# Second feed-forward products as seven block products on one core of a Trainium2 chip

## The chip, the cores and the metric

The kernel runs on one core of one Trainium2 chip. The metric is the device time of one execution in microseconds (us). Before the change the median of three runs is 2907.16 us (2906.84 to 2908.7).

Engines are named as in the profile: PE is TensorE's matmuls, PEld its weight loads, DVE is VectorE, ACT is ScalarE, POOL is GpSimd, SP is SyncE, whose queue issues nearly all DMAs of this kernel.

## The reference

One layer of a decoder trunk on 1024 prompt tokens and 64 sample tokens (8 sequences of 8), all in float32: a half-step feed-forward, a token mixing (pooling branch and a state-space branch), a second half-step feed-forward, and a final norm. What the change touches are the two feed-forwards:

```python
def swiglu(x, w_in, w_out):
    gu = x @ w_in                                   # (tokens, 1024) @ (1024, 2 * 2816)
    g, u = gu[..., :D_FF], gu[..., D_FF:]
    return (jax.nn.silu(g) * u) @ w_out             # (tokens, 2816) @ (2816, 1024)

x = x + 0.5 * swiglu(rmsnorm(x, norm_ffn1[l]), ffn1_w_in[l], ffn1_w_out[l])
...                                                 # token mixing
x = x + 0.5 * swiglu(rmsnorm(x, norm_ffn2[l]), ffn2_w_in[l], ffn2_w_out[l])
```

The product with w_in is called the first product below, the one with w_out the second.

## The kernel before

**Layout.** Activations lie with features on the 128 partitions and tokens along the free dimension. Tokens are split into two halves: half 0 has 512 (prompt), half 1 has 576 (512 prompt and the 64 sample tokens). A tile of one half is one block of 128 features. The hidden width of 2816 is 22 blocks (NFF), the model width 1024 is 8 (KD).

**Precision.** A float32 product is made of three matmuls in a rounded float32 type: the operand and the weight are each split into a high and a low part, and high x high, high x low and low x high are added up in PSUM. `split` (line 354) makes the parts of an operand: ScalarE copies the high part, VectorE subtracts. `load_w` (line 272) loads 4 blocks of weights, 256 KB, and does the same for them (lines 295 and 296). `part` (line 306) does this ahead for chosen chunks and stores the two parts in DRAM, from where load_w later only loads them.

**First products.** `ffn` (line 650) runs one feed-forward. The first few hidden blocks go by `ffn_in_plain` (line 613). All others go by `ffn_in` (line 538), which makes the gate block and the up block of one hidden block by seven products in place of eight; its weights need sums of weight blocks that GpSimd makes (line 438), then the split (lines 444 and 445). The result of one hidden block and one half, g, is stored in DRAM (`hdram`; lines 579, 609 and 627). Its tiles come from a tag of 17 buffers (`fx`, line 109): two results, and t and v, which hold products that were taken out of PSUM. The last hidden block is done half after half.

**Second products.** The loop that begins under `finish(side)` in `ffn` does half 0, then half 1. It loads the 22 operand tiles of the half (`hr`, `hp`, line 682), splits them, and goes over the 8 output blocks m: for each it loads w_out four row blocks at a time and does 22 x 3 matmuls for each piece of the half (half 0 is one piece of 512 columns, half 1 two pieces of 288). PSUM has eight banks; six of them have the tag "pd", which these products and the first ones share. An output block leaves PSUM by one VectorE instruction for each piece (line 700), which adds half of it to the residual tile loaded from `xspill`. The first two output blocks go together, and their weights were prepared by `part` during the first products (`out01`). After half 0 the chain that follows (`after`) is started: after the first feed-forward this is the norm of half 0 for the token mixing; after the second it is the final norm and output, whose first part (`half`) starts when four output blocks are there. The same follows for half 1.

**What sets the order.** Instructions are put on the engines' queues by a scheduler when the program is built; it takes them in program order where their operands and buffers are free. Side work is written as generators ("chains"): each pause names a number of microseconds of TensorE time after which it goes on, and `tick()` in the matmul loops steps the chains that are due. `high_priority` lets a group of instructions be taken earlier: weight splits by HP (40), emptying of PSUM by HP_EV (60).

## Time and profile before

The profiled execution spans 2904.2 us from the first to the last instruction; the median of the runs is 2907.16 us, 2.96 us longer, which is what lies around the span. All times of stages and single instructions are from this one execution.

| stage of the profiled execution (us from the start of the span) | length |
|---|---|
| first feed-forward: plain blocks and operands, 0 to 104.9 | 104.9 |
| first feed-forward: first products, 104.9 to about 524.9 | 420 |
| first feed-forward: second products, half 0, 524.9 to 649.08 | 124.18 |
| first feed-forward: second products, half 1, 649.08 to 790.83 | 141.75 |
| token mixing, to 2146.5 | 1355.7 |
| second feed-forward: plain blocks, to 2207.4 | 60.9 |
| second feed-forward: first products, to 2618.7 | 411.3 |
| second feed-forward: second products, half 0, to 2748.0 | 129.30 |
| second feed-forward: second products, half 1, to 2888.6 | 140.60 |
| last final norm and output, to the end | 15.6 |

How to read the lines shown below: a line of the table by stage has the stretch, its length, then for each engine its busy time and the number of its instructions, then the granted clock of TensorE (1.00 is full), the share of time in which the 16 DMA engines were busy, and GB/s moved. A line of a group has the line of the program, the engine, the operation, output<-inputs by the program's names, shapes, the count; behind the bar the busy time in us and the mean of one in ns; behind the second bar the time that the engine sat idle just before them, and what ended it. All matmuls have the line of the helper that issues them (164), so they are told apart by the names of their tiles: pw for first products, po for second ones. The recorded length of a matmul includes its passage through the array; how often one starts is read from the starts of a row of them.

### The profile page before, as it was taken

The numbers are of one execution on the slowest core, as the hardware profiler recorded it, in microseconds if no ns is written. First come the engines' busy times: TensorE is split into PE (matmuls) and PEld (weight loads), VectorE is DVE, ScalarE is ACT, GpSimd is POOL, SyncE is SP. The second block draws the span as 40 slices with busy tenths as digits, with TensorE's granted clock in tenths as the row PEclk, the third lists the DMA queues.
The fourth block names the chain that finished last, engine by engine and source line by source line (L and its number), as shares of the span: only waits on it lengthen the run. The fifth ranks groups of instructions, "written<-read, shape, count | busy, mean of one in ns | idle before, by whom it ended". The sixth has DMA issues, their size and how long they took to land. (4 is left out here: it accounts for less than half of the span.)

```text
span 2904.2 us, 52545 instructions
## 1 busy us (share of the span) xinstructions
PE 2823.4 (97%) x19306; PEld 2609.3 (90%) x19306; DVE 1701.8 (59%) x2702; ACT 1365.2 (47%) x3004; POOL 1003.0 (35%) x1088
## 2 busy tenths in 40 slices
PE   7999999999999999999999999899999999999998
PEld 6999999789989999999988887678999999997898
DVE  6665555534384586766766777765665544453432
ACT  5454444323354565554556566566234444442322
POOL 5444444000132365564622343332244444440000
PEclk9999999999999999999999999999999999999999
DMA  4575554856445455543376677786764522236642
GB/s 120 166 225 188 170 171 129 280 178 200 125 129 165 151 182 169 190 136 121 106 248 206 197 232 232 256 256 184 255 231 144 163 92 82 79 114 206 220 155 73
DMA packets 520803, 502.84 MB, mean 173 GB/s; under 512 B 36565, under 2 KB 365129, under 8 KB 520537
## 3 DMA queue, kind: packets, MB, share of 16 engines
q1 hardware_dynamic: 520528, 499.47, 54.0%
q8 instruction: 152, 2.49, 0.4%
q14 instruction: 107, 0.87, 0.1%
q10 hardware_dynamic: 16, 0.00, 0.0%
HBM read 356.53 MB, written 143.05 MB: 172 GB/s over the span
## 5 line engine op out<-in xcount | busy, mean ns | idle before, releaser
L164 PE MATMUL pw<-X,wh 128*128 128x288 f32 (+2 forms) x2832 | 625.5, 310 | 2.8 <-ACT t L590 2.6
L164 PEld LDWEIGHTS pw<-X,wh 128*128 128x128 f32 x2832 | 461.3, 189 | 24.5 <-ACT t L590 3.0
L164 PE MATMUL pw<-X,wl 128*128 128x288 f32 (+1 forms) x1644 | 472.9, 288 | 0.9 <-DVE wl L445 0.9
L164 PE MATMUL pw<-hl,wh 128*128 128x256 f32 (+1 forms) x1536 | 391.5, 328 | 0.7 <-ACT t L566 0.7
L445 DVE TENSOR_TENSOR wl<-s,wh 128x512 fp32r<-128x512 f32 x288 | 227.7, 791 | 234.4 <-ACT wh L444 210.7
L164 PE MATMUL pw<-hi,wh 128*128 128x288 f32 x1120 | 331.1, 296 | 0.5 <-ACT t L600 0.5
L164 PE MATMUL pw<-hi,wl 128*128 128x288 f32 x1120 | 330.0, 295 | 0.0
L164 PE MATMUL pw<-lo,wh 128*128 128x288 f32 x1120 | 329.6, 294 | 0.0
L438 POOL TENSOR_TENSOR s<-wraw,wraw 128x512 f32<-128x512 f32 x144 | 196.5, 1365 | 357.3 <-DVE wl L445 253.0
L164 PEld LDWEIGHTS pw<-X,wl 128*128 128x128 f32 x1644 | 311.1, 189 | 1.1 <-DVE wl L445 1.1
L164 PE MATMUL pw<-hl,wl 128*128 128x256 f32 x1072 | 300.0, 280 | 0.0
L296 DVE TENSOR_TENSOR wl<-wraw,wh 128x512 fp32r<-128x512 f32 x208 | 149.6, 721 | 251.1 <-ACT wh L295 248.8
L164 PEld LDWEIGHTS pw<-hl,wh 128*128 128x128 f32 x1536 | 258.8, 189 | 21.7 <-ACT t L566 1.4
L295 ACT ACTIVATE wh<-wraw 128x512 fp32r<-128x512 f32 x208 | 125.5, 605 | 314.6 <-PE po L164 241.7
L444 ACT ACTIVATE wh<-s 128x512 fp32r<-128x512 f32 x288 | 181.0, 630 | 162.4 <-PE pw L164 138.1
L445 DVE TENSOR_TENSOR wl<-wraw,wh 128x512 fp32r<-128x512 f32 x216 | 168.2, 779 | 137.2 <-ACT wh L444 125.6
L164 PEld LDWEIGHTS pw<-hi,wh 128*128 128x128 f32 x1120 | 210.5, 188 | 7.4 <-ACT t L600 1.3
L164 PE MATMUL po<-hh,wh 128*128 128x288 f32 (+1 forms) x800 | 210.8, 323 | 3.6 <-ACT hh L356 3.3
L164 PE MATMUL po<-hr,wh 128*128 128x288 f32 (+1 forms) x800 | 210.9, 323 | 0.0
L164 PE MATMUL po<-hh,wl 128*128 128x288 f32 (+1 forms) x800 | 210.6, 322 | 0.0
L164 PEld LDWEIGHTS pw<-lo,wh 128*128 128x128 f32 x1120 | 210.6, 188 | 0.0
L164 PEld LDWEIGHTS pw<-hi,wl 128*128 128x128 f32 x1120 | 210.1, 188 | 0.4 <-DVE wl L445 0.4
(381 smaller groups left out, 6239.6 us busy)
## 6 DMA issues: line engine op xcount, KB each, us to landing
wraw<-in_ffn_w_in_dram SPq DMA_DIRECT2D x188, 256.0 KB
wh<-part SPq DMA_DIRECT2D x156, 256.0 KB
wl<-part SPq DMA_DIRECT2D x156, 256.0 KB
wraw<-in_w_in_dram SPq DMA_DIRECT2D x144, 256.0 KB
wraw<-in_ffn_w_out_dram SPq DMA_DIRECT2D x120, 256.0 KB
part<-ph SPq DMA_DIRECT2D x80, 256.0 KB
part<-pr SPq DMA_DIRECT2D x80, 256.0 KB
ab<-acsd SPq DMA_DIRECT2D x64, 256.0 KB
```

Source lines behind the costliest of these rows:

```text
L164: T.matmul(out, lhsT, rhs, start=start, stop=stop, skip_group_check=free)
L295: S.activation(wh, raw, AF.Copy)
L296: V.tensor_tensor(wl, raw, wh.bitcast(F32), op=ALU.subtract)
L438: G.tensor_tensor(t, a, b, op=op)
L444: S.activation(wh, a, AF.Copy)
L445: V.tensor_tensor(wl, a, wh.bitcast(F32), op=ALU.subtract)
```

## The change

Hidden blocks are paired: block 2k is the even, block 2k+1 the odd one, eleven pairs (NKK). The 1088 tokens are cut anew into two sides of 544: side 0 is half 0 and the first 32 tokens of half 1, side 1 the other 544. The output blocks are cut into the first four (y = 0) and the last four (y = 1). The product is then 2 x 2 blocks by 2 x 2 blocks, and is done by seven products of block sums, in the order 2, 5, 1, 7, 4, 3, 6, each of 11 row blocks, 4 output blocks and 2 pieces of 272 columns:

- The sums of operands (for products 6, 7, 1, 4, 3) are made by GpSimd in the first products' stage as soon as both blocks of a pair are there for both halves (`sums`), and stored in DRAM (`xq`); the operands of 2 and 5 are stored there straight from g. The result of a hidden block is stored in hdram only by `ffn_in_plain`, from where `sums` loads it again.
- The weight sums (two blocks of w_out each for products 1, 2, 5, 6, 7; one block for 3 and 4) are made by GpSimd when they are needed, and then split (`second_weights`). One load has two row blocks of 256 columns.
- Each group of 2 output blocks has four PSUM banks. A finished bank is added to every residual tile that it belongs to (INTO2: one to two target blocks, with a sign), in two pieces where it lies over the border of the halves. All 16 residual tiles (8 output blocks, 2 halves) stay in fx buffers from product 2 on.
- The operands of the next product are loaded and split during the current one (`fetch_x`); the low parts for products 3 and 6 are made by GpSimd.
- `after` of half 0 is called when product 4 is done, `half` of half 1 after product 3, `after` of half 1 at the end. For the second feed-forward `half` is no longer used for half 0; its final norm and output are one chain.
- The preparation of w_out chunks (`out01`) is gone from both feed-forwards; of the pause before the norm of half 0 (HN_AT), 25, 3 is left.

The diff, without some of the glue:

```diff
-HN_AT, HN_PACE = 25.0, 2.0
+HN_AT, HN_PACE = 3.0, 2.0
+NKK, NQ, NA = NFF // 2, 272, 32
+ORDER2 = "2517436"
+BLOCKS2 = {"1": ((0, 0), (1, 1)), "2": ((0, 1), (1, 1)), "3": ((0, 0),), "4": ((1, 1),), "5": ((0, 0), (1, 0)),
+           "6": ((0, 1), (0, 0)), "7": ((1, 0), (1, 1))}
+MINUS2 = "67"
+INTO2 = {"1": ((0, 0, 1), (1, 1, 1)), "2": ((1, 0, 1), (1, 1, -1)), "3": ((0, 1, 1), (1, 1, 1)),
+         "4": ((0, 0, 1), (1, 0, 1)), "5": ((0, 0, -1), (0, 1, 1)), "6": ((1, 1, 1),), "7": ((0, 0, 1),)}
+IN_PAIRS = "214"
+LO_POOL = "36"
+X_AT, X_PACE = 5.0, 2.2
+SUM_PACE = 1.5
...
-                dma(hdram[0][ff], g[:, : 2 * n])
+                produced(ff, 0, g)
...
-                dma(hdram[h][ff], o["g"][:, : 2 * n])
+                produced(ff, h, o["g"])
...
         dma(hdram[h][ff], g[:, : NTOK[h]])
+        produced(ff, h, g, True)
+
+    def produced(ff, h, g, spilled=False):
+        made[ff, h] = None if spilled else g
+        kk, odd = divmod(ff, 2)
+        if odd:
+            if h == 1:
+                dma(xq["5"][kk], g[:, NA : NA + 2 * NQ])
+        elif h == 0:
+            dma(xq["2"][kk][:, :512], g[:, :512])
+        else:
+            dma(xq["2"][kk][:, 512 : 512 + NA], g[:, :NA])
+        if odd and all((2 * kk + i, q) in made for i in range(2) for q in HALVES):
+            summing.append(start(sums(kk), SUM_PACE))
+
+    def sums(kk):
...
+        def both(p, out, x0, x1, y, op):
+            G.tensor_tensor(out[:, a], x0[:, a], y[:, b0], op=op)
+            G.tensor_tensor(out[:, s], x1[:, :NA], y[:, b1], op=op)
+            dma(xq[p][kk], out[:, :n])
+
+        both("6", fx(name="s6"), e0, e1, e1, ALU.add)
+        yield SUM_PACE
+        both("7", fx(name="s7"), o0, o1, o1, ALU.add)
+        yield SUM_PACE
+        both("1", fx(name="s1"), e0, e1, o1, ALU.add)
+        yield SUM_PACE
+        G.tensor_tensor(o0[:, a], o0[:, a], e0[:, a], op=ALU.subtract)
+        G.tensor_tensor(o0[:, s], o1[:, :NA], e1[:, :NA], op=ALU.subtract)
+        dma(xq["4"][kk], o0[:, :n])
+        yield SUM_PACE
+        G.tensor_tensor(e1[:, NA : NA + n], e1[:, NA : NA + n], o1[:, NA : NA + n], op=ALU.subtract)
+        dma(xq["3"][kk], e1[:, NA : NA + n])
...
+    def second_weights(wo, p, kp, n2, m0):
+        raws = []
+        for x, y in BLOCKS2[p]:
+            raw = sp.tile([P, 4 * P], F32, tag="wraw", bufs=N_RAW, name=nm("wraw"))[:, : n2 * 2 * P]
+            c0 = (4 * y + m0) * P
+            dma(raw.rearrange("p (k c) -> p k c", c=2 * P),
+                wo.rearrange("(k t p) c -> p t k c", t=2, p=P)[:, x, kp : kp + n2, c0 : c0 + 2 * P])
+            raws.append(raw)
+        with tc.high_priority(hp[0]):
+            if len(raws) > 1:
+                s = stage["p"].tile([P, 4 * P], F32, tag="wsum", bufs=N_S, name=nm("ws"))[:, : n2 * 2 * P]
+                G.tensor_tensor(s, raws[0], raws[1], op=ALU.subtract if p in MINUS2 else ALU.add)
...
+            S.activation(wh, s, AF.Copy)
+            V.tensor_tensor(wl, s, wh.bitcast(F32), op=ALU.subtract)
...
+    def second(wo, after, half):
...
+                dma(t[:, :n], xq[p][kk])
+                S.activation(a[:, :n], t[:, :n], AF.Identity)
+                (G if p in LO_POOL else V).tensor_tensor(t[:, :n].bitcast(F32R), t[:, :n], a[:, :n].bitcast(F32), op=ALU.subtract)
...
+        def add(pt, m, side, c, sign):
+            if side:
+                to = [(1, NA + NQ * c, 0, NQ)]
+            else:
+                to = [(0, 0, 0, NQ)] if c == 0 else [(0, NQ, 0, NQ - NA), (1, 0, NQ - NA, NA)]
+            for h, at, of, w in to:
+                o = C[m, h][:, at : at + w]
+                V.scalar_tensor_tensor(o, pt[:, of : of + w], 0.5 * sign, o, op0=ALU.mult, op1=ALU.add)
...
+        for at, p in enumerate(ORDER2):
+            finish(ahead)
+            if at + 1 < len(ORDER2):
+                last = at + 2 == len(ORDER2)
+                ahead = start(fetch_x(ORDER2[at + 1], range(NKK), 1.6 if last else X_PACE), 14.0 if last else X_AT)
+            for m0 in (0, 2):
+                pts = [[psum("pd", "po") for _ in range(2)] for _ in range(2)]
+                for kp in range(0, NKK, 2):
+                    n2 = min(2, NKK - kp)
+                    W2 = second_weights(wo, p, kp, n2, m0)
+                    for j in range(2):
+                        for k in range(n2):
+                            xh, xl = X[p][kp + k]
+                            for i, (w, x) in enumerate(((0, xh), (0, xl), (1, xh))):
+                                for c in range(2):
+                                    mm(pts[j][c][:, :NQ], W2[w][:, k, j * P : (j + 1) * P], x[:, c * NQ : (c + 1) * NQ],
+                                       start=kp + k == 0 and i == 0, stop=kp + k == NKK - 1 and i == 2)
                             tick()
...
+                with tc.high_priority(HP_EV):
+                    for j in range(2):
+                        for c in range(2):
+                            for y, side, sign in INTO2[p]:
+                                add(pts[j][c], 4 * y + m0 + j, side, c, sign)
+            if p == "4":
+                after(0, [C[m, 0] for m in range(KD)])
+            if p == "3" and half:
+                half(1, [C[m, 1] for m in range(KD)])
+        after(1, [C[m, 1] for m in range(KD)])
```

In product 2 the residual tiles are loaded, four output blocks in each of its two groups, and the sums of the last pair are finished there.

More of the change, by code (lines that the diff above doesn't have):

```diff
@@ L669, in ffn, with fetch_x @@
             finish(side)
-        for h in HALVES:
-            N = NTOK[h]
-            parts = [], []
-            for k in range(NFF):
-                own = k < 4 if h == 0 else not half and k >= NFF - 2
-                if 4 <= k < 4 + N_PAIR and (h == 0 or half):
+        second(wo, after, half)
+    def second_weights(wo, p, kp, n2, m0):
[11 more added lines that the diff above has]
+            else:
+                s = raws[0]
+            wh, wl = (sp.tile([P, 4 * P], F32R, tag=t, bufs=N_W, name=nm(t))[:, : n2 * 2 * P] for t in ("wh", "wl"))
+            S.activation(wh, s, AF.Copy)
+            V.tensor_tensor(wl, s, wh.bitcast(F32), op=ALU.subtract)
+        return [t.rearrange("p (k c) -> p k c", c=2 * P) for t in (wh, wl)]
+    def second(wo, after, half):
+        X, C = {p: [] for p in ORDER2}, {}
+        n = 2 * NQ
+        def fetch_x(p, kks, pace):
+            for kk in kks:
+                if p in IN_PAIRS and kk < N_PAIR:
                     a, t, _ = pair(576, "hp")
@@ L1722, in half2 @@
     def half2(g, xt):
+        finish(fin[-1])
         xf.append(xt)
@@ L1726, in after2, with whole @@
     def after2(g, xt):
+        if g == 0:
+            def whole():
+                xf.append(xt)
+                yield from final_head(0)
+                yield from final(0)
+            fin.append(start(whole(), 2.0))
+            return
         finish(fin[-1])
         fin.append(start(final(g)))
-    ffn(ffn2_w_in[0], ffn2_w_out[0], prep2, after2, half=half2, side=part(ffn2_w_out[0], out01))
+    ffn(ffn2_w_in[0], ffn2_w_out[0], prep2, after2, half=half2)
     for c in fin:
```

57 lines of the change are left out of this document (31 added, 26 removed).

## The prediction

> **What bounds the kernel now.** I read the page first, then the time split at the borders of the feed-forward stages, then the rows of the second products.
>
> ```profile
> span 2904.2 us, 52545 instructions
> ...
> PE 2823.4 (97%) x19306; PEld 2609.3 (90%) x19306; DVE 1701.8 (59%) x2702; ACT 1365.2 (47%) x3004; POOL 1003.0 (35%) x1088
> ...
> PEclk9999999999999999999999999999999999999999
> ```
> ```profile
> core 0: us, PE busy (x) PEld busy (x) DVE busy (x) ACT busy (x) POOL busy (x), PEclk, DMA share, GB/s
> ...
> 104.90:511.00 406.10, 404.98 (x2725) 380.11 (x2724) 234.46 (x385) 193.98 (x425) 185.67 (x173) 1.00 0.55 175
> ...
> 2207.40:2605.00 397.60, 397.25 (x2662) 373.30 (x2661) 203.67 (x323) 172.83 (x361) 185.17 (x175) 1.00 0.34 106
> ...
> 2888.60:2904.20 15.60, 2.47 (x21) 1.85 (x18) 6.50 (x15) 5.54 (x14) 1.17 (x1) 0.70 0.44 151
> ```
>
> TensorE is busy 97% of the span at full granted clock. In the two "first product" stages (104.9 to 511 and 2207.4 to 2605) it idles 1.1 and 0.35 us, while POOL has over half its time free. The second products stand in the answer for the tile po alone:
>
> ```profile
> 524.90:649.08 124.18, 121.88 (x529) 98.66 (x529) 4.82 (x7) 1.00 0.69 220
> 649.08:790.83 141.75, 140.91 (x1057) 140.42 (x1055) 6.42 (x15) 1.00 0.55 168
> 2618.70:2748.00 129.30, 126.65 (x554) 101.51 (x553) 5.52 (x8) 1.00 0.62 199
> 2748.00:2888.60 140.60, 139.25 (x1032) 137.56 (x1031) 5.84 (x15) 1.00 0.40 125
> sum 535.83, PE 528.70 PEld 478.15 DVE 22.60; mean PE 132.17 PEld 119.54 DVE 5.65
> ```
>
> Both second products together take 535.8 us and are full of matmuls. So whatever takes matmuls away here comes off the span, unless another resource then ends last. By code one product issues 22 x 8 x 3 = 528 matmuls of 512 columns (first half) and 1056 of 288 (second half); a few records are missing or stand over a border.
>
> **The matmuls.** The change does 7 block products of 11 x 4 x 3 x 2 = 264 matmuls, each 272 columns wide: 1848 per feed-forward, 3696 in all, in place of 3168. Their spacing is taken between two widths of the trace. The timeline shows 30 matmuls of 512 columns in a row, the first and the last of them here; the chain that ended last shows a run of 486 of 288 columns:
>
> ```profile
> 642.28 0.39 PE L164 MATMUL po<-hh,wh 128*128 128x512 f32 x1
> ...
> 648.85 0.39 PE L164 MATMUL po<-hh,wl 128*128 128x512 f32 x1
> ```
> ```profile
> 2823.82 64.78 PE po L164 x486
> ```
>
> 6.57 us over 29 steps is 226.6 ns; 64.78 over 486 is 133.3 ns. That is 0.4165 ns a column plus 13.4 ns, so 272 columns should start every 126.6 ns: 3696 x 0.1266 = 468 us. **535.8 - 468 = 67.8 us** is the gross gain.
>
> **Start of each second product.** In the table above the first windows leave 124.18 - 121.88 = 2.3 and 129.30 - 126.65 = 2.65 us of TensorE idle, mostly waits for operands read back from DRAM. The first product, "2", needs only even row blocks, stored a whole block ahead, so it has no late round trip; but its weights now need a POOL sum ahead of ScalarE and VectorE. I keep 2.5 us each, 5 us (0 to 10).
>
> **Emptying PSUM.** Six banks stand for "pd"; a group takes four. The first two of the next group are free, the other two must be emptied within the first 12 matmuls of that group (1.52 us), plus the 0.76 us by which the last six matmuls of the old group follow the end of its first pair: 2.28 us. The adds:
>
> ```profile
> L700 DVE SCALAR_TENSOR_TENSOR x<-po,x 128x288 f32<-128x288 f32 x32 | 13.1, 451 | 12.4 <-PE po L164 12.4
> L296 DVE TENSOR_TENSOR wl<-wraw,wh 128x512 fp32r<-128x512 f32 x62 | 42.7, 689 | 79.5 <-ACT wh L295 79.5
> L358 DVE TENSOR_TENSOR hr<-hr,hh 128x576 fp32r<-128x576 f32 x22 | 16.7, 758 | 36.3 <-ACT hh L356 36.2
> L295 ACT ACTIVATE wh<-wraw 128x512 fp32r<-128x512 f32 x62 | 38.9, 629 | 93.3 <-PE po L164 88.4 <-DVE wl L296 2.2 <-issue 2.1
> L356 ACT ACTIVATE hh<-hr 128x576 fp32r<-128x576 f32 x22 | 15.1, 686 | 40.2 <-DMA hr<-hd 35.5 <-PE po L164 4.6
> ```
>
> An add of 288 columns is 0.45 us. The first pair has four or five pieces in most products, at most 5 x 0.45 = 2.25 us: just in time. What can be ahead of them on VectorE is one weight or operand subtraction, 0.69 or 0.76 us. So 0 to 0.8 us a border, and I take 0.3: 26 borders, 8 us. VectorE as a whole has room: per feed-forward 84 weight blocks (14 of them half) about 54 us, 55 operand splits 42 us, 120 add pieces of at most 0.45 us, some 47 us: 143 of 234 us. ScalarE: 84 x 0.63 + 77 x 0.69 = 106 of 234.
>
> **DMA in the second products.** Loads have 256 KB each now:
>
> ```profile
> wraw<-in_ffn_w_out_dram SPq DMA_DIRECT2D x120, 256.0 KB
> ...
> x<-xspill SPq DMA_DIRECT2D x24, 288.0 KB
> ```
>
> After: 12 weight blocks of 2816 KB (34.6 MB), 77 operands of 272 KB (21.4 MB), the residual 4.5 MB: 60.5 MB per feed-forward in 234 us, 258 GB/s. What the queues reach:
>
> ```profile
> 642.28:649.08 6.80, 6.80 (x32) 1.00 1.00 347
> ```
> ```profile
> 525.00:560.00 35.00, 32.76 (x139) 25.25 (x139) 10.75 (x17) 7.99 (x14) 0.83 (x2) 1.00 0.87 289
> ```
>
> 347 GB/s at a share of 1.00; 289 at 0.87. The mean of 258 fits, the start does not: in product "2" fall 5.8 MB of weights, 3.1 of the next operands, 4.5 of residual, 0.8 of its own last operands and 1.7 of the last sums being stored, with "5" another 8.8: 24.6 MB in 66.9 us, 368 GB/s. At 347 that takes 70.9 us, 4 us more; weights loaded some blocks ahead and operands needed only as the product reaches them soften it. I take 2.5 us per feed-forward, 5 us (0 to 8). The Trainium skill ("DMA: Bandwidth & Descriptors", Bandwidth) puts the HBM limit of a core at about 358 GB/s; by it the same bytes take an estimated 68.7 us, 1.8 us more per feed-forward. The 347 of the row is close below it.
>
> **The stage ahead.** POOL gets, per pair of row blocks, four sums in two pieces (512 and 32 columns) and one of 544:
>
> ```profile
> L438 POOL TENSOR_TENSOR s<-wraw,wraw 128x512 f32<-128x512 f32 x144 | 196.5, 1365 | 357.3 <-DVE wl L445 253.0 <-DMA wraw<-in_w_in_dram 60.2 <-DMA wraw<-in_ffn_w_in_dram 42.7
> L947 POOL TENSOR_TENSOR ct<-ct,cm 128x64 f32<-128x64 f32 x72 | 42.0, 583 | 23.3 <-ACT ct L940 20.5 <-POOL ra L1011 0.7
> L771 POOL TENSOR_TENSOR lo<-xn,hi 128x576 fp32r<-128x576 f32 x4 | 6.5, 1634 | 4.9 <-DVE hi L766 4.9
> ```
>
> 4 x (1.365 + 0.583) + 1.634 = 9.4 us, times 11 pairs 104 us per feed-forward: POOL goes from 185.7 to 290 of 406 us. It is not full, and the first row says why a delay should hide: its weight sums wait 253 us for VectorE to give their buffer back, so they run ahead of need. Also removed are the 12 prepared weight chunks per feed-forward (line 306), on ScalarE, VectorE and DMA; TensorE waited for none of it, so they are worth nothing. Added stores stand on SyncE's queue behind the POOL sums, ahead of later weight loads; those have that same lead. I take 1 us per feed-forward, 2 us (0 to 20), because held g tiles and sums now share 17 fx buffers with everything else.
>
> **Moved heads and tail.** The first half's norm and final output now run beside the last two products (66 us), with a budget of pauses of some 40 us; at nothing, and if that cover were short, some 10 us. The tail after the last matmul (15.6 us in the first table) keeps its last-half work: unchanged.
>
> **Sum.** -67.8 + 5 + 8 + 5 + 2 = -47.8 us. Span 2904.2 - 47.8 = 2856.4; the median of the runs, 2907.16, lies 2.96 us above the span, so **2859.4 us, 2860 rounded**.
>
> **Rivals.** (A) *Evictions end last.* VectorE's weight subtraction is held up by POOL, and the adds stand behind it. These are the rows of the first stage:
>
> ```profile
> L445 DVE TENSOR_TENSOR wl<-s,wh x80: 677/692/1677, 106.1 to 506.9; 128x512 fp32r<-128x512 f32 x80
> ```
> ```profile
> L438 POOL TENSOR_TENSOR s<-wraw,wraw x40: 1285/1296/1731, 106.9 to 507.5; 128x512 f32<-128x512 f32 x40
> ```
> The slowest subtraction takes 1.68 us where the middle one takes 0.69: 0.99 us lost, less than one POOL sum of 1.30. If at every border the adds stood behind such a one, each would lose 1.5 us instead of 0.3: 26 x 1.2 = 31 us, 2891. For it: POOL is at work in five of seven products. Against it: the middle value is the undisturbed one, and TensorE idles 1.1 of 406 us in a stage with as much POOL. The Trainium skill ("SBUF — State Buffer", Who interferes with whom) says that a VectorE instruction with two SBUF inputs and a GpSimd instruction reading SBUF exclude one another, the later waiting for the whole of the other; the long maximum agrees, and the rule speaks for this rival. 0.13.
>
> (B) *DMA holds the start.* If the traffic gets only the 289 GB/s of the 35 us row, the 24.6 MB take 85 us, 18 more than the matmuls, 15.5 more than I allow: twice that is +31, 2891. The whole stage would be slower than before only under 60.5 MB / 268 us = 226 GB/s. Against: that row's share is 0.87, not full. 0.10.
>
> (C) *272 columns cost what 288 do.* 3696 x 6.7 ns = +25, 2885. Only two widths carry my line. 0.05.
>
> (D) *Slower: the fx buffers.* In the first products each pair now holds its four g tiles into the next pair, and three sums after them until they are stored, out of 17 buffers that also take the five of the block under work and the chunk preparation. If a block finds no buffer for its first evicted bank, TensorE waits for POOL's sums. The gain is used up at 47.8 / 22 = 2.2 us per pair; at one whole POOL round, 4 us, it is 22 x 4 - 47.8 = +40, 2947. For it: nothing else lengthens tile lives so much. Against: 9.4 us of sums in a pair that lasts some 40 us, so I count about 14 tiles at the worst moment. 0.07.
>
> **How the numbers follow.** Forecast 0.65, A 0.13, B 0.10, C 0.05, D 0.07. The forecast's own range: all extra costs at zero gives 2907.2 - 67.8 = 2839, unlikely in full, so 2845; the upper ends of start and DMA give 2868. To leave out no more than 2 in 10 it must reach A, B and C: 2845 to 2895. About 0.2% (6 us) is what a measurement of this kernel can tell from no change. Faster by more: forecast, A, B and C less some tail, 0.89; within 0.2%: 0.03; slower 0.08.
>
> **What would show it.** Right: tile po with 3696 matmuls of 272 columns, about 127 ns apart, the two second products near 243 us each, POOL near 290 us in the first stage with TensorE idle there still under 3 us. Wrong: idle before po released by VectorE's adds at each group border (A); released by ScalarE's wh behind DMA in the first 67 us, DMA share 0.99 (B); spacing of 133 ns (C); idle in pw released by ScalarE's t, the copies that need an fx buffer (D). A first stage grown by over 10 us, or second products over 255 us each, would refute the sum.

## The result and the profile after

The changed kernel takes 2960.45 us (median of 4 runs, 2957.79 to 2961.45) beside 2907.53 us for the kernel before (4 runs, 2906.84 to 2908.7): ratio 1.0175, 95% interval 1.0163 to 1.0186. The change makes the kernel 53 us slower; the forecast was 47 us faster.

First the page of the changed kernel: span, busy time of the engines, and the clock that TensorE was granted in 40 slices.

```profile
span 2958.9 us, 54612 instructions
...
PE 2804.2 (95%) x19834; PEld 2623.6 (89%) x19834; DVE 1869.3 (63%) x2916; ACT 1394.9 (47%) x3070; POOL 1429.9 (48%) x1450
...
PEclk9999999999999999999999999899999999998999
```

TensorE's busy time fell by 19 us (2823.4 to 2804.2) while the span grew by 54.7: it now waits for something. Next the same split by stage as in the prediction (stretch, length, busy time of PE, PEld, DVE, ACT, POOL with counts, granted clock, DMA share, GB/s). The first row is the first products of the first feed-forward over the same 406 us as before; the others are its second products, then both stages of the second feed-forward in full.

```profile
104.90:511.00 406.10, 379.29 (x2480) 354.84 (x2479) 215.47 (x340) 167.36 (x377) 243.47 (x235) 0.97 0.52 169
565.10:836.10 271.00, 245.84 (x1862) 240.72 (x1861) 182.44 (x279) 100.96 (x177) 132.92 (x102) 0.97 0.76 245
2255.20:2672.20 417.00, 411.50 (x2747) 386.31 (x2746) 226.09 (x332) 176.79 (x374) 284.83 (x272) 1.00 0.36 116
2672.20:2943.10 270.90, 250.31 (x1902) 245.97 (x1901) 159.40 (x267) 97.00 (x177) 116.93 (x90) 0.96 0.68 218
```

In the first row TensorE is busy 379.29 of 406.10 us at a clock of 0.97, where it had been 404.98 at 1.00. Between the first starts of the tiles pw, po and the next stage's, the lengths are:

| stage | before | after | change |
|---|---|---|---|
| first feed-forward, first products | 420.1 | 460.6 | +40.5 |
| first feed-forward, second products | 265.8 | 271.0 | +5.2 |
| token mixing and plain blocks | 1416.5 | 1419.1 | +2.6 |
| second feed-forward, first products | 411.1 | 417.0 | +5.9 |
| second feed-forward, second products | 270.2 | 271.1 | +0.9 |

With -0.4 ahead of the first row this is the whole +54.7. So there are two questions: why the first stage grew by 40 us where 1 was expected, and why the second products, which should have shrunk to 243, did not shrink.

Only part of this is waiting. The whole first stage of the changed kernel is this row:

```profile
104.50:565.10 460.60, 430.37 (x2814) 401.83 (x2813) 255.89 (x394) 196.19 (x436) 281.23 (x269) 0.97 0.52 168
```

Before, as many matmuls (2814) kept TensorE busy for 417.82 us at a clock of 1.00 (104.9 to 524.9 us). So of the 40 us, 28 are new idle time, and 12.6 are the same matmuls taking longer at the clock of 0.97.

**The first stage.** These are TensorE's waits of the changed kernel from 105 to 570 us (engine, tile, who was waited for: us in total, times, longest):

```profile
PE ptr L179 <- DMA xin<-in_x_prompt_dram: 10.6, 3, 6.1
PE ptr L179 <- DMA xin<-in_x_sample_dram: 7.5, 2, 5.0
PE pw L175 <- DVE t L579: 5.1, 3, 4.2
PE pw L175 <- DVE t L613: 3.0, 1, 3.0
```

And those of SyncE's queue, from 105 to 560 us:

```profile
SPq L674 <- POOL s L673: 101.3, 31, 6.6
```

Before, TensorE's longest wait in this stage was 1.1 us, none of it for a load. Now it waits 18.1 us for input blocks (xin), which a side chain transposes during this stage, and 8.1 us for VectorE's copies out of PSUM. SyncE stands 101 us behind GpSimd's sums (L673 makes the last piece, L674 stores it); that wait is new. One wait of 4.15 us, followed back in the timeline (start, length, engine, line, in brackets the idle time before and what ended it):

```profile
313.70 1.75 POOL L672 TENSOR_TENSOR s<-g,g 128x512 f32<-128x512 f32 x1
315.42 0.25 POOL L673 TENSOR_TENSOR s<-g,g 128x32 f32<-128x32 f32 x1
...
315.69 0.32 SPq L674 DMA_DIRECT2D xq<-s  x1
316.06 0.43 SPq L321 DMA_DIRECT2D pr<-in_w_o_dram  x1
...
319.12 0.63 ACT L367 ACTIVATE ph<-pr 128x512 fp32r<-128x512 f32 x1 [6.28 <-DMA pr<-in_w_o_dram]
...
319.84 0.69 DVE L369 TENSOR_TENSOR pr<-pr,ph 128x512 fp32r<-128x512 f32 x1 [5.55 <-ACT ph L367]
320.45 0.68 DVE L579 TENSOR_TENSOR t<-pw,t 128x512 f32<-128x512 f32 x1
...
321.19 0.80 PE L175 MATMUL pw<-hl,wh 128*128 128x512 f32 x1 [4.15 <-DVE t L579]
```

Read it from the bottom: TensorE waits for a bank that VectorE empties at L579; VectorE is held at its split of a prepared chunk (pr), because ScalarE is held at the same chunk; ScalarE waits 6.28 us for the chunk's load; the load was given out at 316.06, right behind a store that had stood until GpSimd finished the sum at 315.67. Nobody needs the chunk soon. It stops TensorE because, on every queue of these rows, the instructions behind stand until the one ahead has gone.

Waits of the stores alone do no such harm. In the first products of the second feed-forward (2255 to 2672 us) they are as long:

```profile
SPq L674 <- POOL s L673: 108.6, 31, 6.6
```

GpSimd is as busy there (284.83 of 417.00 us, third row of the split by stage), yet TensorE idles only 5.5 us. That stage transposes no input blocks and prepares no chunks.

**The second products.** They begin with a gap. SyncE's part of the timeline, then TensorE's waits from 565 to 836 us:

```profile
575.96 0.32 SPq L684 DMA_DIRECT2D xq<-g  x1
577.26 0.32 SPq L687 DMA_DIRECT2D xq<-g  x1
577.63 3.77 SPq L774 DMA_DIRECT2D x<-xspill  x8
...
581.93 2.04 SPq L738 DMA_DIRECT2D wraw<-in_ffn_w_out_dram  x3
```
```profile
PE po L175 <- ACT wh L748: 12.9, 3, 10.1
PE po L175 <- DVE x L784: 7.2, 10, 3.1
PE po L175 <- POOL hr L766: 2.4, 2, 1.5
```

The stores of the last pair's sums wait for GpSimd, eight loads of residual tiles follow them, and only at 581.93 come the next weights; TensorE waits 10.1 us for them. The second feed-forward has the same gap (10.7 us). The waits in the list are 22.5 us of the 271.

Here too the clock has a share: against e12 below, where most of what surrounds the matmuls is left out, TensorE is busy 8 and 10 us longer in the two stages (245.84 beside 237.43 us, 250.81 beside 241.01 from the first to the last matmul), for the same number of matmuls within 1, at clocks of 0.97 and 0.96 in place of 1.00.

### The profile page after: what moved, and what is told of

The parts are those of the page before. It is cut to its first block, busy times and chain, and to the rows that moved or that the text cites. A ratio compares the mean times of both kernels' runs of the same rounds, so it can differ in the third digit from the quotient of the medians.

```text
span 2958.9 us, 54612 instructions
## 1 busy us (share of the span) xinstructions
PE 2804.2 (95%) x19834; PEld 2623.6 (89%) x19834; DVE 1869.3 (63%) x2916; ACT 1394.9 (47%) x3070; POOL 1429.9 (48%) x1450
## 5 line engine op out<-in xcount | busy, mean ns | idle before, releaser
L456 DVE TENSOR_TENSOR wl<-s,wh 128x512 fp32r<-128x512 f32 x288 | 248.4, 864 | 268.5 <-ACT wh L455 250.4
L449 POOL TENSOR_TENSOR s<-wraw,wraw 128x512 f32<-128x512 f32 x144 | 203.0, 1409 | 307.0 <-DVE wl L456 208.5
L456 DVE TENSOR_TENSOR wl<-wraw,wh 128x512 fp32r<-128x512 f32 x216 | 179.6, 832 | 120.1 <-ACT wh L455 116.9
L744 POOL TENSOR_TENSOR ws<-wraw,wraw 128x512 f32<-128x512 f32 x120 | 165.7, 1384 | 166.9 <-DMA wraw<-in_ffn_w_out_dram 103.8
L175 PE MATMUL po<-hh,wh 128*128 128x272 f32 x848 | 184.8, 298 | 31.4 <-ACT wh L748 22.1
L175 PEld LDWEIGHTS pw<-hl,wl 128*128 128x128 f32 x1072 | 204.1, 190 | 0.0
L455 ACT ACTIVATE wh<-wraw 128x512 fp32r<-128x512 f32 x216 | 135.3, 627 | 138.9 <-PE pw L175 115.0
L175 PE MATMUL po<-hr,wh 128*128 128x272 f32 x848 | 180.4, 294 | 6.6 <-POOL hr L766 6.6
```

Of the source, the lines that this page charges most:

```text
L175: T.matmul(out, lhsT, rhs, start=start, stop=stop, skip_group_check=free)
L449: G.tensor_tensor(t, a, b, op=op)
L455: S.activation(wh, a, AF.Copy)
L456: V.tensor_tensor(wl, a, wh.bitcast(F32), op=ALU.subtract)
L744: G.tensor_tensor(s, raws[0], raws[1], op=ALU.subtract if p in MINUS2 else ALU.add)
```

## The experiments

Each kernel is the changed one with the edit named, unless another base is named, and ran once beside a run of the kernel before on the same chip, unless more is said. Stages: F1, S1 are first and second products of the first feed-forward, F2, S2 of the second (changed kernel: 460.6, 271.0, 417.0, 271.1; before: 420.1, 265.8, 411.1, 270.2). F2 of e3 and e12 to e15, whose code for that stage is one and the same, lies between 412.7 and 418.8 us, so differences of less than 6 us in a stage are hardly to be read.

**e1: all operand stores on GpSimd's queue.**

```diff
-            dma(xq[p][kk], out[:, :n])
+            G.dma_start(xq[p][kk], out[:, :n])
```


> The stores of the operands for the second products are issued on POOL's own queue, behind the sums that they wait for, in place of SyncE's. Theory S (SyncE's queue: the stores wait there for POOL's sums, and the loads behind them come late): the first products of the first feed-forward go from 460.6 us to under 430, those of the second from 417 to about 412, the whole to about 2920 or less. Rival F (the 17 fx buffers are short, because g tiles and sums are held): the first products stay over 450. Rival P (POOL is too slow for sums and weight sums): over 455, as POOL has the issue of the stores as well.

Measured: 2957.74 us; F1 459.1, S1 260.3, F2 434.7, S2 257.8. The gap at the start of the second products is gone (-11 and -13), the first stages are not better. VectorE's weight subtractions got longer: their mean in F1 goes from 928 to 1343 ns (rows in the last section). And loads of input blocks now wait for a stored sum to give back its buffer (16.6 us, twice, 10.0 at the longest), which the changed kernel doesn't show. Taking SyncE out of the way by giving GpSimd more to do doesn't tell the queue from GpSimd's work, but it shows that the stores' place on SyncE's queue alone isn't the whole cause.

**e2: the residual loads of each group two steps later.**

```diff
-                    if at == 0 and kp == 2:
+                    if at == 0 and kp == 6:
```


> Only product 2 is changed: the end of the last sums and the loads of the residual are placed two weight blocks later (after the fourth instead of the second load of weights). Theory S: the two waits of 10 us at the start of the second products (weights behind eight residual loads and the stores on SyncE's queue) fall to under 4 us each, and the second products from 271 to about 263 us each; the first products stay as they are, so about 2944. Rival D (DMA is full there, the order is no matter): both second products stay within 3 us of 271.

Measured: 2966.03 us; F1 461.4, S1 275.0, F2 418.4, S2 267.6. Nothing gained. The order of the residual loads does make the one long wait: the longest for a weight is now 3.8 us in S1 and 4.2 in S2 (10.1 and 10.7 before this edit). But as much time is waited for weights in several pieces, 11.1 and 11.5 us beside 12.9 and 11.8: the order only spreads it.

**e3: no operand sums.** The stores stay with the same bytes, from tiles of g; the sums are left out.

```diff
-            G.tensor_tensor(out[:, a], x0[:, a], y[:, b0], op=op)
-            G.tensor_tensor(out[:, s], x1[:, :NA], y[:, b1], op=op)
-            dma(xq[p][kk], out[:, :n])
+            dma(xq[p][kk], y[:, NA : NA + n])
```


> The sums on GpSimd are left out: in place of each sum a piece of 544 columns of one g tile is stored, so the stored operands are not those of the reference's product; as many bytes go to DRAM, and the g tiles are still held until their pair is complete. Theory S: the stores wait for nothing, the first products of the first feed-forward take under 430 us. Rival F: the g tiles are held as before and only three of seven held tiles are gone, so 440 or more. Rival P: about 420, but then the stores on POOL's queue would not help.

Measured: 2905.24 us; F1 425.2, S1 262.2, F2 417.6, S2 261.7. The sums are worth 35 us of F1 and 9 of each second product, and nothing of F2 (417.0 with them). But even with the sums for nothing, the kernel is only level with the one before: the second products are 12 us shorter than before, where 50 were forecast, and the first products are 12 us longer.

**e4: one weight block.** The second block of each weight sum is left out; GpSimd adds the first one to itself.

```diff
-        for x, y in BLOCKS2[p]:
+        for x, y in BLOCKS2[p][:1]:
```


> Of the two weight blocks of products 1, 2, 5, 6 and 7 only the first is loaded and added to itself, so the second block is missing from the result; 14.4 MB of 60.5 are not moved in each second product. Rival D (DMA holds the second products): they go from 271 us to under 255 each. If the losses come from the order on SyncE's queue at the start and from VectorE and POOL later: 262 to 268, since only the loads that are late by volume come earlier.

Measured: 2936.67 us; F1 464.1, S1 261.2, F2 416.1, S2 257.3. With 14.4 MB less in each, the second products give 10 and 14 us, the wait for weights at the start among them. Both lie between the two expectations.

**e5: each store of a sum given out 4.5 us of TensorE time later.**

```diff
-            dma(xq[p][kk], out[:, :n])
+            later(4.5, lambda: dma(xq[p][kk], out[:, :n]))
```


> Change: the store of each sum is put on SyncE's queue 4.5 us of TensorE time later than in the changed kernel, when GpSimd should be done with the sum; GpSimd does all the sums. After: first products of the first feed-forward 460.6 us (420.1 before), the 19 waits of that store for GpSimd 58 us. If the loads are late because they stand behind waiting stores (queue theory): the store's waits fall under 15 us and the stage to 435 us or less. If what costs is GpSimd's work itself, which holds up VectorE's two-input instructions: the waits fall as well, but the stage stays at 450 to 465. If the 17 buffers held too long cost it: each sum is held 4.5 us longer, so the stage is at least as long as after, 460 to 475.

Measured: 2934.48 us; F1 449.8, S1 263.9, F2 419.0, S2 265.0. F1 gives 11 us and each second product 6 to 7, but the waits of the stores only went from 101 to 85 us (the 58 us of the expectation are those up to 400 us), so this run doesn't do what it was to do. It speaks for the queue, without deciding.

**e6: tiles, stores and bytes as they were, but GpSimd adds only 32 columns of each sum.** Most of the operand sums are left out.

> Change: the tiles of the sums are taken and held as in the changed kernel and the stores have the same bytes, but GpSimd adds only 32 columns of each sum (512 of the last one); the other columns are stored as they are, so most of the operand sums are left out. Buffers held too long (F): the stage of first products of the first feed-forward stays at 450 or more, since every tile of the changed kernel is still there. GpSimd's time, or waits behind it (G): it falls to about 425, as with no sums at all (425.2). Second products without late sums in front of them: about 262 each, as with no sums (262.2, 261.7).

Measured: 2904.82 us; F1 428.6, S1 261.6, F2 417.0, S2 259.5. The same tiles are taken for sums and stored, and F1 is 32 us shorter, so their number alone (rival D) doesn't make the loss. But the tiles are given back sooner, since the small sums are done sooner: how long GpSimd holds them isn't tested here.

**e7: no weight sums in the second products.** Both blocks are loaded; the first is used alone.

```diff
-                G.tensor_tensor(s, raws[0], raws[1], op=ALU.subtract if p in MINUS2 else ALU.add)
+                s = raws[0]
```


> Change: in the second products both weight blocks are loaded, but GpSimd's weight sum is left out and the first block used alone; operand sums as in the changed kernel. After: second products 271.0 and 271.1 us, floor of 1848 matmuls at 126.6 ns 234. If GpSimd's weight sums hold VectorE up (exclusion): both second products fall by 12 us or more beyond their start waits, to 255 or less. If the transfers set it (same bytes as after): they stay at 265 to 272. First products unchanged, 460 and 417.

Measured: 2935.56 us; F1 459.7, S1 257.6, F2 414.0, S2 266.4. S1 falls by 13 us, between the two expectations; S2 by 5, within the second. Start waits of 7 us are left in both.

**e8: no chunk preparation in the first feed-forward's first products.** The chunks are split later, where they are used.

> Change: the preparation of weight chunks (two parts stored ahead in DRAM) no longer runs during the first products of the first feed-forward; those chunks are loaded and split where they are used, so nothing is left out. If the sums hurt only because they meet this side work, which adds subtractions on VectorE and tiles to the 17 buffers: the stage of first products falls from 460.6 to 430 or less, and the stages behind it grow by up to 20 us. If the sums alone are too much: it stays above 450.

Measured: 2956.87 us; F1 438.6, S1 271.4, F2 414.0, S2 267.3, token mixing 1445.7. Half of the loss of F1 (22 us) needs the side work to be there; it is given back in the token mixing (+26.6). F1 lies between the two expectations: the transposes of input blocks are still there, and TensorE waits 11.6 us for their loads. The second feed-forward has neither side work, and its first products lost only 5.9 us with the same sums, which stay without them (e3).

**e9: longer leads.** Input blocks are loaded one block ahead, chunks 8 us ahead.

```diff
-PART_AT, PART_W, PART_PACE = 20.0, 4.0, 3.0
+PART_AT, PART_W, PART_PACE = 20.0, 8.0, 0.0
...
-                t = fx(name="xin2")
-                dma(t[:c, :512], src[:, q * 512 : (q + 1) * 512])
+                t = got.pop(0)
+                if todo:
+                    got.append(load(*todo.pop(0)))
```


> Change: the changed kernel, but each load of an input block (xin) is given out one block ahead of its transposes and the load of a chunk to be prepared 8 us ahead in place of 4 (the pause behind it gone). Sums, stores and their queue stay. After: first products of the first feed-forward 460.6 us; of its waits 18.1 us of TensorE are for xin. If the sums hurt because these loads, given out only 4 us of TensorE time ahead, come late behind waiting stores (short leads): the xin waits fall under 4 us and the stage to 440 or less. If GpSimd's work as such slows VectorE (exclusion): the stage stays at 450 or more. If the buffers are what is short: two more tiles are held, so 460 or more.

Measured: 2942.86 us; F1 449.6, S1 269.4, F2 417.3, S2 270.1. TensorE's waits for xin fall from 18.1 to 0.5 us, but F1 by only 11, since waits for VectorE's copies (t) rise from 8.1 to 10.5 us and some for ScalarE's are added. With 449.6 us F1 lies between the first two expectations. Short leads are where part of the delay came out; the rest finds other ways.

**e10: the five operand sums of a pair on VectorE.**

```diff
-            G.tensor_tensor(out[:, a], x0[:, a], y[:, b0], op=op)
+            E = V if p in SUM_V else G
+            E.tensor_tensor(out[:, a], x0[:, a], y[:, b0], op=op)
```


> Change: the changed kernel with all five operand sums of a pair on VectorE in place of GpSimd (about 55 instructions of 512 or 544 columns and 44 of 32 in each feed-forward); tiles and stores stay. After: stage of first products 460.6 and 417.0. If GpSimd, by waits behind it and by holding up VectorE, is what the sums cost: the stage falls to 435 or less in the first feed-forward, though VectorE has some 50 us more. If it is the tiles and transfers of the sums: it stays above 450. If VectorE has no room for them beside the copies out of PSUM: both stages grow, the second over 425.

Measured: 2912.46 us; F1 434.2, S1 263.7, F2 413.5, S2 263.8. Same tiles, stores, bytes and queue: 48 us come back only because VectorE makes the sums and not GpSimd. The stores' waits on SyncE's queue shrink with it (46.4 us behind VectorE's sums, 101.3 behind GpSimd's), so this run doesn't tell the queue from GpSimd's work either. The rows by stretch, the changed kernel first, then e10:

```profile
160.00:260.00 100.00, 88.44 (x569) 82.06 (x568) 52.70 (x93) 39.52 (x96) 52.90 (x53) 0.95 0.65 211
```
```profile
160.00:260.00 100.00, 94.88 (x620) 87.88 (x619) 68.47 (x121) 45.88 (x111) 40.71 (x38) 0.97 0.69 229
```

VectorE has 16 us more in these 100 us and GpSimd 12 less, and TensorE does 51 matmuls more. VectorE, before the change the busier of the two (234 us beside 186 in the 406 us of the prediction's row), was the better place.

**e11: the leads of e9, the later stores of e5, and LO_POOL = "" (low parts of products 3 and 6 on VectorE).**

> Change: the leads of the run e9, the stores of the sums 4.5 us later as in e5, and the low parts for products 3 and 6 on VectorE in place of GpSimd. If short leads and the queue make the first stage's loss: 430 or less there (449.8 with later stores alone), 262 in each second product, about 2905 in all. If GpSimd's work itself: the stage stays at 445 or more, about 2925.

Measured: 2921.8 us; F1 443.5, S1 260.3, F2 416.7, S2 260.8. The leads and the later stores together give 17 us of F1, which ends nearer to the second expectation than to the first. The moved low parts belong to the second products, which are 3.6 and 4.2 us below those of e5, less than the spread named above.

**e12: bare second products.** From e3: one weight block, no weight sums, and each bank added to one residual tile only; all matmuls stay.

```diff
-                            for y, side, sign in INTO2[p]:
+                            for y, side, sign in INTO2[p][:1]:
```


> Change: no operand sums, one weight block loaded in place of two and no weight sums, and each finished bank added to one residual tile only: parts of the computation left out, all matmuls kept. It asks what is left of the second products when most of what is around them is gone; 1848 matmuls at 126.6 ns are 234 us. If transfers, weight sums and adds make the loss together: 236 to 243 each. If a start and a moved norm make it (or the matmuls cost more in a row than 126.6): 250 or more.

Measured: 2858.35 us; F1 422.5, S1 240.9, F2 415.3, S2 242.1. Two stretches of S1:

```profile
525.00:560.00 35.00, 35.00 (x279) 35.00 (x278) 20.00 (x40) 15.37 (x27) 1.01 (x1) 1.00 0.99 336
577.70:604.00 26.30, 26.30 (x210) 26.30 (x210) 14.86 (x27) 11.29 (x19) 0.00 (x0) 1.00 0.64 204
```

279 matmuls in 35.00 us are 125.4 ns each, beside the 126.6 forecast. So the matmuls do run as forecast, and their gain is lost to what the seven products need around them. It is smaller than forecast, though: the two stages together are 53 us below the kernel before (483.0 beside 536.0), not 67.8.

**e13, e14, e15: one of the three taken away, each on the base e3** (S1 262.2, S2 261.7). e13: each bank added once. e14: no weight sums, both blocks loaded. e15: one block, added to itself.

> Change, on the run without operand sums (e3: second products 262.2 and 261.7): each finished bank is added to one residual tile only, so half of the adds of products 1, 2, 3, 4 and 5 are left out. If the emptying of PSUM makes what is left of the loss (adds): both second products 250 or less. If transfers or weight sums make it: 257 or more.

> Change, on the run without operand sums (e3: 262.2 and 261.7): both weight blocks are loaded, GpSimd's weight sum is left out, the first block used alone. If GpSimd's sums hold up VectorE's weight split and the adds behind it (exclusion): 250 or less. If transfers make the loss: 257 or more.

> Change, on the run without operand sums (e3: 262.2 and 261.7): one weight block is loaded in place of two and added to itself, so GpSimd's sum stays and 14.4 MB per feed-forward go. If the transfers of the start and of product 5 make the loss: 250 or less, and the first 35 us of each without a wait for weights. If the adds or the weight sums make it: 257 or more.

Measured: e13 2894.91 us, S1 255.3, S2 263.9; e14 2885.7 us, S1 254.8, S2 257.8; e15 2887.48 us, S1 255.7, S2 252.6. None reaches 250 in both. In S1 each is worth 6.5 to 7.4 us; the three add up to 20.8 and all at once (e12) give 21.3. In S2 the single ones give -2.2 (e13), 3.9 and 9.1, 10.8 in all, against 19.6 together. No single one of them is the bound. With one run of each, single terms of 4 to 7 us are hardly above the spread named above; only the sum of all three is clear.

**e16: e10 with the leads of e9 and LO_POOL = ""**.

> Change: all operand sums on VectorE (as in e10), the longer leads of e9, and the low parts for products 3 and 6 on VectorE; nothing left out. By the sizes of e10 (434.2, 413.5; 263.7, 263.8), e9 (xin waits of 7 us gone) and e11 (second products 260.5): first stage 426, second products 260.5 each, in all 2895 to 2900, faster than before by 0.2 to 0.4%. If VectorE has no room for the low parts beside the sums: 2910 or more.

Measured: 2901.58 us (10 runs, 2898.9 to 2905.19) beside 2905.91 (13 runs): ratio 0.9985, interval 0.9975 to 0.9994. F1 423.1, S1 262.1, F2 415.7, S2 260.8. The time is 1.6 us above the expected 2895 to 2900; the best complete version found is about 4 us below the kernel before, less than the 0.2% that count as a difference here.

**e17: e11 with the stores 10 us later.**

> Change: the run e11 with each store of a sum 10 us of TensorE time later in place of 4.5, so that GpSimd should be done with the sum when SyncE comes to its store; all sums still on GpSimd. In e11: first stage 443.5, 18 us of TensorE idle there, the stores' waits for GpSimd 82 us; with the sums on VectorE and the same leads 423.1 (e16). If what is left is the loads behind waiting stores (queue): the waits fall under 25 us and the stage to 430 or less. If it is GpSimd's work itself, by the subtractions that it stretches: the waits fall and the stage stays at 440 to 446. If buffers held 5.5 us longer are short: over 446, with waits for the stores' landing.

Measured: 2919.29 us; F1 447.5, S1 259.3, F2 419.5, S2 256.1. The stores still wait 81.6 us, so the later time in the program doesn't move them behind the sum on the queues. This run tells nothing on the queue. F1 is over the 446 us that were to show short buffers, but the waits for a store's landing are 6.7 us in all (7.5 in the changed kernel), and 4 us more than in e11 are not to be read.

**e18: e16, and GpSimd does sums into a tile that nobody reads.**

```diff
+            G.tensor_tensor(d[:, a], e0[:, a], e0[:, a], op=ALU.add)
+            G.tensor_tensor(d[:, s], e0[:, s_e], e0[:, s_e], op=ALU.add)
```


> Change: the run e16 (sums on VectorE, longer leads; first stage 423.1 and 415.7) and beside each sum two instructions of 512 and 32 columns on GpSimd, into a tile that nobody reads: GpSimd has the work of the changed kernel again, but no store waits for it, and nothing is left out. If the loads behind waiting stores make the remaining 20 us (queue): the first stage stays at 430 or less. If GpSimd's work itself makes them, by holding up VectorE's subtractions and its own products for the blocks: 438 or more, with the mean of VectorE's wl near 900 ns (747 in e16), though VectorE, with the sums, has less room than in the changed kernel.

Measured: 2981.32 us; F1 475.2, S1 262.9, F2 438.7, S2 264.6: +52.1 and +23.0 in the first products, though no store waits for these sums. One wait of it in the timeline:

```profile
401.83 1.48 POOL L681 TENSOR_TENSOR dm<-g 128x512 f32<-128x512 f32 x1
...
403.27 1.27 POOL L566 TENSOR_TENSOR g<-g 128x256 f32<-128x256 f32 x1
...
404.57 0.42 ACT L572 ACTIVATE g<-g 128x256 f32<-128x256 f32 x1 [8.53 <-POOL g L566]
...
405.23 0.56 ACT L574 COPY v<-pw 128x512 f32<-128x512 f32 x1
...
405.85 0.80 PE L176 MATMUL pw<-X,wh 128*128 128x512 f32 x1 [4.33 <-ACT v L574]
```

GpSimd has a part of the block's own arithmetic (L566 adds two halves of g). It stands behind the sums; ScalarE's next activation waits 8.53 us for it; the copy of a PSUM bank stands behind that activation; TensorE waits for the bank. Here GpSimd's work is enough without a store that waits. But it is not the wait of the changed kernel: for the copy at this place (L573 there) its TensorE waited 0.3 us in F1, here 27.1. And F2 grew to 438.7 us, where the changed kernel, with as much work on GpSimd, takes 417.0: here VectorE makes the sums besides. The expected mean of wl near 900 ns is not reached (828 ns): in this wait it is not VectorE's subtraction that carries the delay but ScalarE's place in the order.

## Why the prediction was wrong

**The failed step** is the stage ahead: "Added stores stand on SyncE's queue behind the POOL sums, ahead of later weight loads; those have that same lead. I take 1 us per feed-forward, 2 us (0 to 20)". The stage grew by 46.4 us (40.5 and 5.9). Without the sums 35 of the 40.5 go and none of the 5.9 (e3). Three things in the step were wrong. The weight loads do have that lead, but on the same queue stand input blocks and chunks that are loaded 4 us of TensorE time before they are used (18.1 us of waits for input blocks, gone in e9). A late chunk stops ScalarE and VectorE, which also empty PSUM, in order. And "it is not full" was read from a mean: GpSimd did get the work that was counted (281 of 460 us; 290 of 406 were forecast), but a mean doesn't show what stands behind a single sum: here a store, and behind it the load of a chunk; in e18 a part of the block itself. Cause shown: GpSimd making the sums (e3, e6, e10, e16), in a stage that has side work; the second feed-forward, with the same sums, the same waits of the stores and no such side work, loses nothing to them (417.0 us with the sums, 417.6 without), and F1 without the chunks loses 22 us less (e8). For the transposes of input blocks, the other side work, it is argued from their waits. How the 40 us split into the queue behind the stores and the work on GpSimd is not settled: the queue was seen at work in single waits and e9 with e5 gives 17 us (e11), the work alone can cost more than that (e18, only in a kernel where VectorE makes the sums too), and the runs that were to take the store waits away (e5, e17) left them at 82 to 85 us.

**The gross gain is mis-sized.** 535.8 us is the whole of the old stages, with their idle time and some other matmuls; 468 us is matmuls alone. By the prediction's own spacings the old matmuls take 2 x (528 x 226.6 + 1056 x 133.3 ns) = 520.8 us, so like for like 52.9 us go, which is what e12 leaves (53). The sum adds 5 of the missing 15 back as the start; 10 us of the forecast were never there.

**Right:** the matmuls (125.4 ns against 126.6; rival C falls), the order of size of the waits for adds (7.2 and 2.8 us against 8 in all), and the tail (15.6 us both times). **Too small:** the start, 2.5 us each, has single waits of 10.1 and 10.7 us, and the granted clock falls beside them. The DMA backlog, 5 us in all, is 6.5 and 9.1 us by e15, part of it that same start. **Not in the sum:** the weight sums on GpSimd, 7.4 and 3.9 us by e14, which the prediction had only as a rival. So the second products take 271 us each and not 243, and 262 without the operand sums; the 12 us that they then gain are lost in the first products, so that the change would not have paid even with the operand sums for nothing (e3: 2905.24 us). **At nothing without a reason:** the clock. The sum priced waits and no matmul that runs slower beside them, which is 12.6 us of F1 and 8 and 10 us of the second products.

**The rivals.** D named the right stage and side, with 2947 for 2960, but its own sign, waits for ScalarE's t, makes 2.3 us of F1 (2.2 before), and e9, which holds two more tiles, is 11 us faster. Waits for a stored tile to land are 5.1 us on ScalarE and 2.4 on GpSimd. So too few buffers is not what made the loss; that the long hold adds a little to it is not excluded. A and B each hold a part: adds, weight sums and transfers share the second products' loss, and none of them ends last throughout. The two signs that were to refute the sum, a first stage grown by over 10 us and second products over 255 us, both came.

## What to carry to other kernels

When work is put on an engine "with room", list who waits for that engine's other results and what stands behind those waits on each in-order queue; a mean busy share says nothing on that (GpSimd was busy 61% of F1, and 68% of F2, where no cost of its sums was found). Look for loads with the shortest lead on the queue that gets new waits, since they, not the far-ahead weights, show the delay. And cost a product with fewer multiplications by all that goes with it: operand sums, two weight blocks in place of one, weight sums, doubled adds and the clock ate the gain one small term at a time. Compare like with like, too: matmuls with matmuls, or stage with stage.

## What the runs showed of the hardware that was not expected

VectorE's instructions with two operands in SBUF stretch with GpSimd's load, those with one operand in PSUM don't. Groups of F1 in the changed kernel, then in e1 (105 to 560 us; behind the first bar busy us and mean ns):

```profile
L456 DVE TENSOR_TENSOR wl<-s,wh 128x512 fp32r<-128x512 f32 x83 | 76.8, 928 | 80.7 <-ACT wh L455 78.2 <-POOL s L449 1.4 <-issue 0.5
...
L568 DVE TENSOR_TENSOR g<-pw,t 128x512 f32<-128x512 f32 x19 | 13.0, 682 | 0.6
```
```profile
L456 DVE TENSOR_TENSOR wl<-s,wh 128x512 fp32r<-128x512 f32 x82 | 109.5, 1343 | 62.5 <-ACT wh L455 59.7 <-PE ptr L179 2.4
...
L568 DVE TENSOR_TENSOR g<-pw,t 128x512 f32<-128x512 f32 x19 | 12.9, 681 | 0.5 <-PE pw L175 0.2
```

And one instruction can be held through several of GpSimd's, here four in a row in e1 (spans on POOL are rough):

```profile
300.93 3.52 DVE L456 TENSOR_TENSOR wl<-s,wh 128x512 fp32r<-128x512 f32 x1 [0.34 <-ACT wh L455]
```
```profile
301.13 0.27 POOL L683 TENSOR_TENSOR g<-g,g 128x32 f32<-128x32 f32 x1
301.34 1.29 POOL L449 TENSOR_TENSOR s<-wraw,wraw 128x512 f32<-128x512 f32 x1
302.59 1.30 POOL L672 TENSOR_TENSOR s<-g,g 128x512 f32<-128x512 f32 x1
303.84 0.71 POOL L673 TENSOR_TENSOR s<-g 128x32 f32<-128x32 f32 x1
```

The Trainium skill ("SBUF — State Buffer", Who interferes with whom) says that the later of the two waits for the whole of the other. The trace agrees that the one holds up the other (the middle one of these subtractions in e1 takes 0.72 us), but 3.52 us is more than any one of these four.

The granted clock falls where TensorE has stood still: in the 30 us with the 10 us gap the row below shows 0.83 and 17.57 us of matmuls, while e12, without the gap, has 1.00 at the same place. So a wait costs more than its length: over F1 the same 2814 matmuls are busy 430.37 us at 0.97 and 417.82 at 1.00, a ratio of 1.03, the same as that of the clocks.

```profile
565.10:595.20 30.10, 17.57 (x120) 16.75 (x121) 0.00 (x0) 0.83 0.70 237
```
